# Sliding-window attention of the second block by pairs of heads, each pair behind its own query projection

## The chip, the cores and the metric

The kernel runs on one core of a Trainium2 chip. Of the core's engines TensorE (PE) does the matrix products, VectorE (DVE) and ScalarE (ACT) the element-wise work, GpSimd (POOL) a little of it, and SyncE (SP) issues most of the transfers. The metric is the device time of one execution in microseconds, the median of several runs.

## The reference, cut to what matters

Two blocks follow one another: the first with four branches (2 layers of it), the second with a feed-forward part, a mixer and another feed-forward part. The change lies in the mixer of the second block, with 512 positions and 1024 features:

```python
h = modulate(rms_norm_2(x, g_pre_mix[l]), sh2, sc2)
proj = h @ w_in[l]
q = proj[..., :D_ATTN].reshape(bsz, s, N_Q_HEADS, HEAD_DIM)            # 8 heads of 64
k = proj[..., D_ATTN:D_ATTN + D_KV].reshape(bsz, s, N_KV_HEADS, HEAD_DIM)   # 2 heads of 64
v = proj[..., D_ATTN + D_KV:D_ATTN + 2 * D_KV].reshape(bsz, s, N_KV_HEADS, HEAD_DIM)
u = proj[..., D_ATTN + 2 * D_KV:]                                      # 512 columns
attn = sliding_window_attention(q, k, v, attn_sinks[l])
ssm = s5_ssm(u, ...)
mixed = jnp.concatenate([rms_norm_2(attn, g_attn_out[l]), rms_norm_2(ssm, g_ssm_out[l])], axis=-1)
mixed = mixed @ w_out[l]
```

In the attention, each block of 128 queries reads its own block of 128 keys and the one before it (the first block only its own). A bias by distance is added, the maximum takes a sink in, and the softmax runs over the keys and the sink:

```python
m = jnp.maximum(jnp.max(scores, axis=-1, keepdims=True), sink)
p = jnp.exp(scores - m)
p = p / (jnp.sum(p, axis=-1, keepdims=True) + jnp.exp(sink - m))
out = jnp.einsum('bnkgqj,bnjkd->bnqkgd', p, vv)
```

The norm behind it (`rms_norm_2(attn, ...)`) runs over all 512 columns of a position, so over all eight heads. `s5_ssm` is a linear recurrence over the positions, with a GELU and a gate `y * sigmoid(y @ w_glu + b_glu)` behind it.

## The kernel before

Features lie on the partitions, positions along the free axis. A product of the large kind is split in three: an fp32 operand is kept as a rounded part and a remainder, and lines 258, 259 and 260 multiply high by high, low by high and high by low. The splits of the weights are made by ScalarE (L218) and VectorE (L219), from tiles `wr` into tiles `wh`, some of them with names of their own (`wa`).

The mixer of the second block is built in `block2`. First `mixer_in` projects `u` (tiles `ut`), `k` (`kd`), `v` (`vT`) and the first 128 columns of `q`, which are two heads. Then two generators are woven into one another, which means that the program text of one is emitted in steps between the steps of the other:

- `mixer`, the recurrence: four groups of products with `us` (L2347: 128 partitions, 64 moving columns, plain fp32), each followed by VectorE's multiplications and eight scans (L2348 to L2353); then four groups of output products (L2364 to L2366) with the GELU behind them; then the gate: products of `y2h` and `y2l` with a weight of 512 rows (lines 258 to 260, 512 columns), a tanh, L2397 and the splits L2405.
- `window_attention`: the three other projections of `q` (24 products with 512 columns each, two heads each), then a loop over the four blocks of queries. `scores(b)` makes the scores of all eight heads of a block (L2438, from `ho`, the keys, and `q`), adds the bias and takes the minimum of the negated scores on VectorE (L2441), and runs the softmax up to the reciprocal of the sum (`softmax_sink`). `values(b)` transposes the exponentials (L2453), copies them out of PSUM on ScalarE, multiplies them with the values (L2459) and scales by the reciprocal (L2462) into a tile `ot` of its block. `result(b)` squares and sums `ot` (L2469), takes a reciprocal square root by three Newton steps of short VectorE instructions (L2470, L268 to L275), scales (L2473), transposes (L2476) and splits the result (L2480 on ScalarE, L2481 on VectorE) into the tiles that the output projection reads. The three parts are staggered: scores of block i, values of block i - 1, result of block i - 2.

When both are done, `attended` multiplies the attention's columns with the first half of `w_out` (weights `wa` first). It begins with the columns of query blocks 0 and 1 and reads all eight heads. The other half of `w_out` follows.

The text's order is not the final one. A class `Plan` takes all instructions of the kernel, with costs and dependencies of its own, and writes a new order for every engine. What stands next to what on an engine is therefore read from the built kernel, as below, not from the text.

Of the kernel before, what the change touches and what calls it, by code (L numbers as in the profile page):

```python
# [11 lines left out]
F32 = mybir.dt.float32  # L12
# [4 lines left out]
AF = mybir.ActivationFunctionType  # L17
ALU = mybir.AluOpType
PSUM = bass.MemoryType.PSUM
DRAM = bass.MemoryType.DRAM  # L20
P = 128
NT = 528
NM = 16
# [13 lines left out]
KC = 8  # L37
BIG = 3.0e38
# [21 lines left out]
def free_bc(ap, n):  # L60

    return ap[:, :, None].to_broadcast([ap.shape[0], ap.shape[1], n])
# [57 lines left out]
class Net:  # L120
# [615 lines left out]
    def p_transposes(self, Ps, k0, n, pool, ch):  # L736
# [4 lines left out]
        for i in range(n):  # L741
            for h in range(2):
                nc.tensor.transpose(ps[:, (2 * i + h) * P:(2 * i + h + 1) * P], Ps[h][:, k0 + i * P:k0 + (i + 1) * P], self.ident)
        PT = pool.tile([P, 512], F32, tag=f"PT{ch}", name=f"PT_{self.n}", bufs=2)
        self.alt_copy(PT[:, :2 * n * P], ps[:, :2 * n * P])
        return PT.rearrange("p (i h q) -> p i h q", i=2, h=2)

# [12 lines left out]
    def pv_block(self, Ps, b_first, n_blocks, vt, vm, pool, kvs, ch=""):  # L760
# [5 lines left out]
        with self.in_turn():  # L766
            po = self.pst("o")
            for p in range(0, H, 2):
# [7 lines left out]
                for i in range(0, n_blocks, 2):  # L776
                    n = min(2, n_blocks - i)
                    PT = self.p_transposes(Ps[p:p + 2], NM + i * P, n, pool, ch)
                    if i == 0:
# [3 lines left out]
                    for k in range(n):  # L783
                        for s in range(2):
                            self.turn = nc.tensor.matmul(o[s], lhsT=vt[:, b_first + i + k, kv[s]:kv[s] + 64], rhs=PT[:, k, s], start=False,
                                                         stop=(i + k == n_blocks - 1), tile_position=(0, 64 * s), skip_group_check=True)
# [26 lines left out]
    def pv_meta(self, Pt, nk_blocks, vt, vm, r, pool, ch=""):  # L813
# [3 lines left out]
        with self.in_turn():  # L817
# [5 lines left out]
            for i in range(nk_blocks):  # L823
                nc.tensor.transpose(pt[:, i * P:(i + 1) * P], Pt[:, NM + i * P:NM + (i + 1) * P], self.ident)
            PT = pool.tile([P, 512], F32, tag=f"PT{ch}", name=f"PT_{self.n}", bufs=2)
            self.alt_copy(PT[:, :nk_blocks * P], pt[:, :nk_blocks * P])
# [984 lines left out]
class Net2(Net):  # L1811
# [598 lines left out]
    def window_attention(self, pool):  # L2410
        nc, I = self.nc, self.ins
        V, G = nc.vector, nc.gpsimd
        W = I["w_in_2"][0]
        kd, vT, q = self.kd, self.vT, self.q2
        vt = pool.tile([P, 4, P], F32, tag="vt2", name="vt2")
        ps = self.pst("t")
        for b in range(4):
            nc.tensor.transpose(ps[:, b * P:(b + 1) * P], vT[:, b * P:(b + 1) * P], self.ident)
        nc.scalar.copy(vt, ps.rearrange("p (b f) -> p b f", b=4))
        for c in range(1, 4):  # L2420
            self.mm(self.wload(W[:, P * c:P * c + P], KC), 0, self.ux, KC, NM, self.qev[c])
            yield
        bias = pool.tile([P, 2048], F32, tag="alibi", name="alibi").rearrange("p (h k) -> p h k", h=8)
        nc.sync.dma_start(bias, I["c_alibi"].rearrange("p (h k) -> p h k", h=8))
        sink = pool.tile([P, 8], F32, tag="sink2", name="sink2")
        nc.sync.dma_start(sink, I["attn_sinks_2"].to_broadcast([P, 8]))
        for c in range(4):
            self.mixed[c] = (self.xtile("u", F32R), self.xtile("u", F32R))
        def scores(b):
            k0, nk, b0 = (0, 128, 128) if b == 0 else (P * (b - 1), 256, 0)  # L2430
            nm = self.small(8, "nm8")
            sb = []
            for h in range(8):
                hp = (h % 2) * 64
                if h % 2 == 0:
                    bank = self.pst("s")
                s = bank[:, 256 * (h % 2):256 * (h % 2) + 256]
                nc.tensor.matmul(s[:, :nk], lhsT=q[h // 2][hp:hp + 64, b * P:(b + 1) * P], rhs=kd[h // 4][hp:hp + 64, k0:k0 + nk],  # L2438
                                 start=True, stop=True)
                t = pool.tile([P, 256], F32, tag="sb2", name=f"sb2_{b}{h}", bufs=15)  # L2440
                V.tensor_tensor_reduce(out=t[:, :nk], in0=s[:, :nk], in1=bias[:, h, b0:], scale=-1.0, scalar=BIG,  # L2441
                                       op0=ALU.add, op1=ALU.min, accum_out=nm[:, h:h + 1])
                sb.append(t)
            return sb, self.softmax_sink(sb, nk, nm, sink, 8, "W"), nk // P, k0 // P

        def values(b, sb, r, nb, kb):
            po = self.pst("o")
            for hh in range(0, 8, 2):
                pt = self.pst("t")
                for h in (hh, hh + 1):  # L2450
                    for i in range(nb):
                        o = (2 * (h - hh) + i) * P
                        nc.tensor.transpose(pt[:, o:o + P], sb[h][:, i * P:(i + 1) * P], self.ident)  # L2453
                PT = pool.tile([P, 2, 256], F32, tag="PT2", name=f"PT2_{b}{hh}", bufs=2)
                nc.scalar.copy(PT[:, :, :nb * P], pt.rearrange("p (h k) -> p h k", h=2)[:, :, :nb * P])
                for h in (hh, hh + 1):
                    kv = (h // 4) * 64
                    for i in range(nb):
                        nc.tensor.matmul(po[:, h * 64:h * 64 + 64], lhsT=PT[:, h - hh, i * P:(i + 1) * P],  # L2459
                                         rhs=vt[:, kb + i, kv:kv + 64], start=(i == 0), stop=(i == nb - 1))  # L2460
            ot = pool.tile([P, 512], F32, tag="ot2", name=f"ot2_{b}", bufs=2)
            V.tensor_tensor(out=ot.rearrange("p (h d) -> p h d", h=8), in0=po.rearrange("p (h d) -> p h d", h=8),  # L2462
                            in1=free_bc(r, 64), op=ALU.mult)
            return ot

        def result(b, ot):
            sq = pool.tile([P, 512], F32, tag="vT2", name=f"sqw{b}")
            v = self.small(1, "vw")
            nc.scalar.activation(sq, ot, AF.Square, accum_out=v)  # L2469
            V.tensor_scalar(out=v, in0=v, scalar1=1.0 / 512, scalar2=1e-6, op0=ALU.mult, op1=ALU.add)  # L2470
            rr = self.small(1, "rw")
            self.rsqrt(v, rr, 1)
            V.tensor_scalar(out=ot, in0=ot, scalar1=rr, scalar2=None, op0=ALU.mult)  # L2473
            ps = self.pst("t")
            for c in range(4):
                nc.tensor.transpose(ps[:, c * P:(c + 1) * P], ot[:, c * P:(c + 1) * P], self.ident)  # L2476
            for c in range(4):
                hi, lo = (t[:, NM + b * P:NM + (b + 1) * P] for t in self.mixed[c])
                p, g = ps[:, c * P:(c + 1) * P], self.col["g_attn_out"][:, c:c + 1]
                nc.scalar.activation(hi, p, AF.Copy, scale=g)  # L2480
                V.scalar_tensor_tensor(out=lo, in0=p, scalar=g, in1=hi.bitcast(F32), op0=ALU.mult, op1=ALU.subtract)  # L2481

        st, ot = {}, {}
        for i in range(6):
            if i < 4:
                st[i] = scores(i)
                yield
            if 0 < i < 5:
                ot[i - 1] = values(i - 1, *st[i - 1])
                yield  # L2490
            if i > 1:
                result(i - 2, ot[i - 2])
                yield

    def block2(self, taps=None):
        nc, I = self.nc, self.ins
# [580 lines left out]
```

## Time and profile before

| | |
|---|---|
| time, median of 3 runs | 3325.56 us (3321.98, 3325.56, 3337.65) |
| the profiled execution's own time | 3333.74 us |
| its span, first to last instruction | 3332.0 us |
| mean granted clock of TensorE | 0.948 |
| TensorE busy (products) | 3146.6 us, 94% |
| VectorE, ScalarE, GpSimd busy | 1856.6 us (56%), 1278.9 us (38%), 416.9 us (13%) |

The profile describes one execution. "Busy" says only that an engine was executing something; how fast TensorE went while busy is told by the granted clock, of which 1.0 is the full 2.4 GHz and 0.5 is 1.2 GHz. The end of a product is modelled, since products overlap in the engine; what one costs in a row of others is read from the start of one to the start of the next.

### The profile page before, as it was taken

To read this page: it belongs to the slowest core of one execution; us is meant where nothing else is said; L and a number is where in the kernel's file an instruction comes from. 1 tells how busy PE (TensorE), PEld (TensorE's weight loads), DVE (VectorE), ACT (ScalarE), POOL (GpSimd) and SP (SyncE) were. 2 spreads that over 40 slices of the span, in tenths; PEclk is the share of its full clock that TensorE was granted. 3 is DMA by queue.
4 is the path that set the end of the run, shared out by engine and by line. 5 is a ranking of instruction groups with operands and counts; after the bars stand their busy time and mean duration, and the time that the engine had idled before them with its cause. 6 is when DMAs were issued, how large, how long until landed. Compare 5 with 4: busy or idle time off the path is not lost. (4 is left out here: it accounts for less than half of the span.)

```text
span 3332.0 us, 57805 instructions
## 1 busy us (share of the span) xinstructions
PE 3146.6 (94%) x21892; PEld 2761.1 (83%) x21892; DVE 1856.6 (56%) x5062; ACT 1278.9 (38%) x2856; POOL 416.9 (13%) x444
## 2 busy tenths in 40 slices
PE   7888999999999988999999999999999999989997
PEld 6777888999999976877678887798888988888887
DVE  4466588754645857568965555853223634642224
ACT  2356444333332345654433232243323514433332
POOL 0101000011110011200002112411110201211101
PEclk9889999999999988999999999989999976889998
DMA  4721223343544652123344444572333543233343
GB/s 138 175 51 45 72 77 88 110 124 106 160 126 120 192 141 58 37 80 95 94 130 145 130 139 137 179 231 83 95 111 116 159 135 98 74 108 95 93 124 95
DMA packets 645883, 380.41 MB, mean 114 GB/s; under 512 B 66500, under 2 KB 613884, under 8 KB 645476
## 3 DMA queue, kind: packets, MB, share of 16 engines
q1 hardware_dynamic: 628520, 365.22, 37.6%
q0 software_dynamic: 13632, 9.61, 1.9%
q8 instruction: 172, 2.82, 0.4%
q10 hardware_dynamic: 3452, 1.89, 0.3%
q14 instruction: 107, 0.88, 0.1%
HBM read 333.16 MB, written 45.52 MB: 114 GB/s over the span
## 5 line engine op out<-in xcount | busy, mean ns | idle before, releaser
L258 PE MATMUL ps_mm<-u,wh 128*128 128x256 f32 (+2 forms) x2928 | 971.0, 333 | 16.8 <-ACT g L1514 4.4
L260 PE MATMUL ps_mm<-u,wh 128*128 128x256 f32 (+2 forms) x2928 | 963.6, 331 | 0.6 <-POOL u L231 0.3
L259 PE MATMUL ps_mm<-u,wh 128*128 128x256 f32 (+2 forms) x2912 | 956.7, 330 | 4.8 <-DVE wh L219 4.8
L258 PEld LDWEIGHTS ps_mm<-u,wh 128*128 128x128 f32 x2928 | 563.9, 193 | 74.1 <-issue 10.4
L219 DVE TENSOR_TENSOR wh<-wr,wh 128x512 fp32r<-128x512 f32 (+1 forms) x531 | 367.3, 703 | 460.3 <-issue 228.1
L218 ACT ACTIVATE wh<-wr 128x512 fp32r<-128x512 f32 (+1 forms) x588 | 354.9, 619 | 699.1 <-PE ps_mm L259 267.4
L260 PEld LDWEIGHTS ps_mm<-u,wh 128*128 128x128 f32 x2928 | 563.4, 193 | 50.7 <-issue 4.7
L259 PEld LDWEIGHTS ps_mm<-u,wh 128*128 128x128 f32 x2912 | 561.0, 193 | 53.5 <-DVE wh L219 6.2
L259 PE MATMUL ps_mm<-hid,wh 128*128 128x256 f32 (+2 forms) x988 | 298.3, 310 | 3.2 <-DVE wh L219 3.1
L258 PE MATMUL ps_mm<-hid,wh 128*128 128x256 f32 (+2 forms) x948 | 287.4, 312 | 2.8 <-ACT wh L218 2.8
L260 PE MATMUL ps_mm<-hid,wh 128*128 128x256 f32 (+2 forms) x948 | 287.1, 311 | 0.0
L1846 DVE SCALAR_TENSOR_TENSOR acc<-ho,cact,acc 128x128 f32<-128x128 f32 x504 | 186.4, 373 | 37.7 <-DMA ho<-in_w_ada_dram 30.1
L259 PEld LDWEIGHTS ps_mm<-hid,wh 128*128 128x128 f32 x988 | 184.4, 190 | 15.7 <-DVE wh L219 4.5
L258 PEld LDWEIGHTS ps_mm<-hid,wh 128*128 128x128 f32 x948 | 177.9, 191 | 13.4 <-ACT wh L218 3.0
L260 PEld LDWEIGHTS ps_mm<-hid,wh 128*128 128x128 f32 x948 | 177.6, 191 | 9.7 <-issue 0.4
L231 POOL TENSOR_TENSOR hid<-g,hid 128x512 fp32r<-128x512 f32 (+1 forms) x85 | 92.4, 1088 | 682.5 <-ACT hid L230 682.5
L218 ACT ACTIVATE wh<-wrx 128x512 fp32r<-128x512 f32 (+1 forms) x160 | 96.0, 601 | 205.0 <-PE ps_mm L260 100.8
L219 DVE TENSOR_TENSOR wh<-wrx,wh 128x512 fp32r<-128x512 f32 (+1 forms) x131 | 87.4, 667 | 136.7 <-issue 116.4
L88 POOL TENSOR_TENSOR na<-na,g 128x256 f32<-128x256 f32 (+2 forms) x62 | 63.1, 1018 | 778.8 <-issue 418.1
L258 PE MATMUL ps_mm<-u,hid 128*128 128x256 f32 (+1 forms) x448 | 135.2, 302 | 16.6 <-ACT hid L218 16.6
L259 PE MATMUL ps_mm<-u,hid 128*128 128x256 f32 (+1 forms) x448 | 135.0, 301 | 5.3 <-DVE hid L219 5.1
L260 PE MATMUL ps_mm<-u,hid 128*128 128x256 f32 (+1 forms) x448 | 133.7, 298 | 0.0
(589 smaller groups left out, 5674.8 us busy)
## 6 DMA issues: line engine op xcount, KB each, us to landing
wr<-in_w_in_dram SPq DMA_DIRECT2D x220, 256.0 KB
ho<-in_w_ada_dram SPq DMA_DIRECT2D x144, 256.0 KB
wr<-in_w_ffn_down_dram SPq DMA_DIRECT2D x80, 256.0 KB
wr<-in_w_down_dram SPq DMA_DIRECT2D x66, 256.0 KB
wr<-in_w_ffn_gate_dram SPq DMA_DIRECT2D x62, 256.0 KB
wr<-in_w_gate_dram SPq DMA_DIRECT2D x61, 256.0 KB
wr<-in_w_ffn_up_dram SPq DMA_DIRECT2D x60, 256.0 KB
wr<-in_w_up_dram SPq DMA_DIRECT2D x60, 256.0 KB
```

The lines of the kernel that those rows point to most:

```text
L88: nc.gpsimd.tensor_tensor(out=acc[:, a:b], in0=acc[:, a:b], in1=sq[:, a:b], op=ALU.add)
L218: self.last_split = nc.scalar.activation(hi[:, i:e], raw, AF.Copy)
L219: (nc.vector if o else eng).tensor_tensor(out=lo[:, i:e], in0=raw, in1=hi[:, i:e].bitcast(F32), op=ALU.subtract)
L231: (eng or self.nc.vector).tensor_tensor(out=lo, in0=x, in1=hi.bitcast(F32), op=ALU.subtract)
L258: T.matmul(o, lhsT=wh, rhs=xh[:, a:b], start=start, stop=False)
L259: T.matmul(o, lhsT=wl, rhs=xh[:, a:b], start=False, stop=False)
L260: T.matmul(o, lhsT=wh, rhs=xl[:, a:b], start=False, stop=stop)
L1846: V.scalar_tensor_tensor(out=acc, in0=w[:, k], scalar=c, in1=acc, op0=ALU.mult, op1=ALU.add)
```

## The change

The loops of the attention change places. The outer loop runs over the four pairs of heads, and the scores, the softmax and the values of a pair are made for all four blocks of queries at once. The projection of the next pair's queries stands behind the values of the pair before it, where all three stood ahead of the loop. The results need all heads of a block, so all four stand behind the loop. The sinks are copied once into a tile of 128 x 32 in the order in which the pairs use them. The finished values go into one tile `ot2` of four blocks by 512 columns, of which a pair writes 128 columns in every block.

```diff
-        for c in range(1, 4):
-            self.mm(self.wload(W[:, P * c:P * c + P], KC), 0, self.ux, KC, NM, self.qev[c])
-            yield
+        yield
...
+        sinks = pool.tile([P, 4, 4, 2], F32, tag="sinks", name="sinks")
+        V.tensor_copy(sinks, sink.rearrange("p (c h) -> p c h", h=2)[:, :, None, :].to_broadcast([P, 4, 4, 2]))
...
+        span = [(0, 128, 128)] + [(P * (b - 1), 256, 0) for b in range(1, 4)]
+
+        def scores(c):
+
             nm = self.small(8, "nm8")
             sb = []
-            for h in range(8):
-                hp = (h % 2) * 64
-                if h % 2 == 0:
-                    bank = self.pst("s")
...
+            for b, (k0, nk, b0) in enumerate(span):
+                bank = self.pst("s")
+                for i in range(2):
+                    h, hp = 2 * c + i, 64 * i
+                    s = bank[:, 256 * i:256 * i + 256]
+                    nc.tensor.matmul(s[:, :nk], lhsT=q[c][hp:hp + 64, b * P:(b + 1) * P], rhs=kd[h // 4][hp:hp + 64, k0:k0 + nk],
+                                     start=True, stop=True)
...
+        ots = pool.tile([P, 4, 512], F32, tag="ot2", name="ot2")
...
+            V.tensor_tensor(out=ots[:, :, P * c:P * (c + 1)].rearrange("p b (h d) -> p b h d", h=2),
+                            in0=po.rearrange("p (b h d) -> p b h d", b=4, h=2),
+                            in1=r.rearrange("p (b h) -> p b h", h=2)[:, :, :, None].to_broadcast([P, 4, 2, 64]), op=ALU.mult)
...
-        st, ot = {}, {}
-        for i in range(6):
-            if i < 4:
-                st[i] = scores(i)
+        st = None
+        for c in range(5):
+            new = scores(c) if c < 4 else None
+            yield
+            if c:
+                values(c - 1, *st)
                 yield
-            if 0 < i < 5:
-                ot[i - 1] = values(i - 1, *st[i - 1])
+            st = new
+            if c < 3:
+                self.mm(self.wload(W[:, P * (c + 1):P * (c + 2)], KC), 0, self.ux, KC, NM, self.qev[c + 1])
                 yield
-            if i > 1:
-                result(i - 2, ot[i - 2])
-                yield
+        for b in range(4):
+            result(b, ots[:, b])
+            yield
```

What this does to the order on TensorE is seen at three places. Each row is one instruction or several alike ("x4"): its line, operation, the tile written and the tiles read, and the size of the output. The first place is the end of the three projections, before the change. `ps_mm_29996` is the third later projection, `ps_s` a score tile, `us` the recurrence's input.

```order
L260 MATMUL ps_mm_29996<-u_28744,wh_29986 128x512
L258 MATMUL ps_mm_29996<-u_28745,wh_29986 128x512
L2438 MATMUL ps_s_30075<-ho_29370,q_0_29373 128x128
L259 MATMUL ps_mm_29996<-u_28745,wh_29987 128x512
L260 MATMUL ps_mm_29996<-u_28746,wh_29986 128x512
L2347 MATMUL ps_mm_29965<-us,wh_29963 128x64 x7
L2438 MATMUL ps_s_30082<-ho_29370,q_1_29374 128x128
L2438 MATMUL ps_s_30089<-ho_29371,q_2_29375 128x128
L2438 MATMUL ps_s_30096<-ho_29371,q_3_29376 128x128
```

Here the last products of the third projection have passed, and the scores of query block 0 (128 columns, with all four tiles of `q`) stand between the first groups of the recurrence. The place that answers to it after the change is the start of the second later projection, `ps_mm_30229`.

```order
L2440 MATMUL ps_s_29909<-ho_29370,q_0_29373 128x256
L2440 MATMUL ps_s_30059<-ho_29370,q_1_29374 128x256
L2347 MATMUL ps_mm_30185<-us,wh_30183 128x64 x8
L2440 MATMUL ps_s_30066<-ho_29370,q_1_29374 128x256
L2418 MATMUL ps_t_29855<-misc,vT_29372 128x128 x4
L2347 MATMUL ps_mm_30198<-us,wh_30196 128x64 x8
L258 MATMUL ps_mm_30229<-u_28731,wh_30219 128x512
L259 MATMUL ps_mm_30229<-u_28731,wh_30220 128x512
L260 MATMUL ps_mm_30229<-u_28732,wh_30219 128x512
```

All four groups with `us` now stand ahead of the second projection, and between them stand scores of the first and the second pair, `q_0` and `q_1` (256 columns for all blocks but the first). The second place is the end of the third later projection after the change, `ps_mm_30472`.

```order
L258 MATMUL ps_mm_30472<-u_28745,wh_30462 128x512
L259 MATMUL ps_mm_30472<-u_28745,wh_30463 128x512
L260 MATMUL ps_mm_30472<-u_28746,wh_30462 128x512
L2469 MATMUL ps_t_30389<-misc,sb_12_30061 128x128 x2
L2469 MATMUL ps_t_30389<-misc,sb_13_30064 128x128 x2
L2364 MATMUL ps_mm_30498<-us,wh_30499 128x64
```

The third projection, with 24 products, has moved behind three of the four groups of output products; behind it transposes of the second pair's exponentials (heads 2 and 3) and the fourth group of output products follow. The third place is on VectorE, at the end of the attention. Before the change, it shows the values of the last query block (`ot_3`) and what follows.

```order
L2462 TENSOR_TENSOR ot_3_30810<-ps_o_30765,rW_30605 128x512
L273 TENSOR_TENSOR rt_5359_30849<-ry_5360_30850 128x1
L219 TENSOR_TENSOR wh_31099<-wr_31100,wh_31098 128x512
L274 TENSOR_TENSOR rt_5359_30849<-rt_5359_30849,rv_5358_30848 128x1
L219 TENSOR_TENSOR wh_31099<-wr_31104,wh_31098 128x512
L275 SCALAR_TENSOR_TENSOR rw_30847<-rt_5359_30849,ry_5360_30850 128x1
L2405 SCALAR_TENSOR_TENSOR u_30820<-g_30818,gs,u_30819 128x8x32
L2473 TENSOR_SCALAR ot_2_30663<-ot_2_30663,rw_30847 128x512
L2470 TENSOR_SCALAR vw_30918<-vw_30918 128x1
```

Here only the results of blocks 2 and 3 follow (the square roots of block 2 are in progress above), with splits of weights and the gate's splits. After the change, the same place begins with the values of the last pair, L2477.

```order
L2477 TENSOR_TENSOR ot_29886<-ps_o_30701,rW_30569 128x4x128
L219 TENSOR_TENSOR wh_30809<-wr_30810,wh_30808 128x512
L2397 SCALAR_TENSOR_TENSOR g_30647<-g_30647,yf 128x512
L2485 TENSOR_SCALAR vw_30775<-vw_30775 128x1
L268 TENSOR_SCALAR rv_5346_30779<-vw_30775 128x1
L269 TENSOR_SCALAR rt_5347_30780<-vw_30775 128x1
L270 TENSOR_SCALAR ry_5348_30781<-rt_5347_30780 128x1
L273 TENSOR_TENSOR rt_5347_30780<-ry_5348_30781 128x1
L274 TENSOR_TENSOR rt_5347_30780<-rt_5347_30780,rv_5346_30779 128x1
L2405 SCALAR_TENSOR_TENSOR u_30649<-g_30647,gs,u_30648 128x8x32
L275 SCALAR_TENSOR_TENSOR ry_5348_30781<-rt_5347_30780,ry_5348_30781 128x1
L2397 SCALAR_TENSOR_TENSOR g_30676<-g_30676,yf 128x512
```

Behind the last values, the result of the first block only begins (L2485 with the square root's steps), and the gates L2397 and their splits L2405 stand between its steps; the results of the three other blocks follow.

## Rows read from the trace of the kernel before

**Rows 1.** Page, 40 slices of the span: tenths of the granted clock.

```profile
PEclk9889999999999988999999999989999976889998
```

**Rows 2.** Stretches: length; busy PE, PEld, DVE, ACT, POOL; clock; DMA share; GB/s.

```profile
2673.30:2698.90 25.60, 25.57 (x138) 21.06 (x136) 6.28 (x27) 4.50 (x7) 0.89 (x1) 1.00 0.47 151
2698.90:2797.90 99.00, 99.00 (x398) 85.24 (x397) 34.92 (x120) 24.44 (x76) 12.24 (x13) 0.50 0.36 111
2797.90:2811.50 13.60, 11.53 (x66) 7.95 (x65) 4.95 (x23) 7.88 (x26) 1.27 (x1) 1.00 0.03 11
2811.50:2818.40 6.90, 6.90 (x25) 6.03 (x25) 5.57 (x18) 5.60 (x12) 1.19 (x1) 0.51 0.12 40
2818.40:2828.60 10.20, 7.57 (x51) 6.55 (x50) 6.94 (x20) 7.75 (x17) 1.85 (x2) 1.00 0.46 132
2828.60:2843.65 15.05, 11.36 (x48) 10.35 (x49) 10.92 (x39) 8.33 (x18) 0.00 (x0) 0.50 0.72 225
2673.30:2843.65 170.35, 161.93 (x718) 137.18 (x717) 69.58 (x243) 58.50 (x154) 17.44 (x17) 0.65 0.38 117
```

**Rows 3.** Timeline of TensorE at full clock: start, duration, instruction.

```profile
2798.34 0.39 PE L259 MATMUL ps_mm<-y2h,wh 128*128 128x512 f32 x1
2798.57 0.40 PE L258 MATMUL ps_mm<-y2h,wh 128*128 128x512 f32 x1
2798.90 0.70 PE L2438 MATMUL ps_s<-ho,q 64*128 64x256 f32 x2
2799.52 0.50 PE L259 MATMUL ps_mm<-y2h,wh 128*128 128x512 f32 x1
...
2821.76 0.60 PE L2476 MATMUL ps_t<-misc,ot 128*128 128x128 f32 x4
2822.20 0.60 PE L2453 MATMUL ps_t<-misc,sb 128*128 128x128 f32 x4
...
2825.12 1.00 PE L2459 MATMUL ps_o<-vt,PT 128*128 128x64 f32 x8
2825.96 0.33 PE L97 MATMUL ps_q<-misc,na 128*128 128x1 f32 x2
```

**Rows 4.** Timeline of TensorE, where the clock fell.

```profile
2695.22 0.71 PE L2438 MATMUL ps_s<-ho,q 64*128 64x128 f32 x6
...
2696.33 0.70 PE L2438 MATMUL ps_s<-ho,q 64*128 64x256 f32 x4
2696.96 1.10 PE L2347 MATMUL ps_mm<-us,wh 128*128 128x64 f32 x8
```

**Rows 5.** Timeline of TensorE, where the clock rose again.

```profile
2787.40 5.38 PE L2459 MATMUL ps_o<-vt,PT 128*128 128x64 f32 x24
2792.54 0.77 PE L258 MATMUL ps_mm<-y2h,wh 128*128 128x512 f32 x1
...
2797.80 0.47 PE L260 MATMUL ps_mm<-y2l,wh 128*128 128x512 f32 x1
```

**Rows 6.** Timeline of TensorE: last values, first product of the output projection.

```profile
2830.55 3.51 PE L2459 MATMUL ps_o<-vt,PT 128*128 128x64 f32 x16
...
2843.65 0.55 PE L258 MATMUL ps_mm<-u,wa 128*128 128x256 f32 x1 [1.50 <-DVE nv L107]
```

**Rows 7.** Timeline of VectorE between 2824 and 2837 us.

```profile
2824.07 0.35 DVE L2481 SCALAR_TENSOR_TENSOR u<-ps_t,col,u 128x128 fp32r<-128x128 f32 x1
2824.33 0.15 DVE L270 TENSOR_SCALAR ry<-rt 128x1 int32<-128x1 int32 x1
...
2834.10 0.69 DVE L2462 TENSOR_TENSOR ot<-ps_o,rW 128x512 f32<-128x512 f32 x1 [2.50 <-PE ps_o L2459]
2834.71 0.15 DVE L273 TENSOR_TENSOR rt<-ry 128x1 f32<-128x1 f32 x1
2834.78 0.68 DVE L219 TENSOR_TENSOR wh<-wr,wh 128x512 fp32r<-128x512 f32 x1
...
2836.71 0.48 DVE L2473 TENSOR_SCALAR ot<-ot,rw 128x512 f32<-128x512 f32 x1
```

More of the change, by code (lines that the diff above doesn't have):

```diff
@@ L2426, in window_attention @@
         nc.sync.dma_start(sink, I["attn_sinks_2"].to_broadcast([P, 8]))
+        sinks = pool.tile([P, 4, 4, 2], F32, tag="sinks", name="sinks")
+        V.tensor_copy(sinks, sink.rearrange("p (c h) -> p c h", h=2)[:, :, None, :].to_broadcast([P, 4, 4, 2]))
         for c in range(4):
             self.mixed[c] = (self.xtile("u", F32R), self.xtile("u", F32R))
-        def scores(b):
-            k0, nk, b0 = (0, 128, 128) if b == 0 else (P * (b - 1), 256, 0)
+        span = [(0, 128, 128)] + [(P * (b - 1), 256, 0) for b in range(1, 4)]
@@ L2431, in scores @@
+        def scores(c):
             nm = self.small(8, "nm8")
             sb = []
-            for h in range(8):
-                hp = (h % 2) * 64
-                if h % 2 == 0:
-                    bank = self.pst("s")
[L2437 to L2443, printed above, removed]
@@ L2444, in scores @@
-            return sb, self.softmax_sink(sb, nk, nm, sink, 8, "W"), nk // P, k0 // P
-        def values(b, sb, r, nb, kb):
+            for b, (k0, nk, b0) in enumerate(span):
[5 more added lines that the diff above has]
+                                     start=True, stop=True)
+                    t = pool.tile([P, 256], F32, tag="sb2", name=f"sb2_{b}{h}", bufs=15)
+                    V.tensor_tensor_reduce(out=t[:, :nk], in0=s[:, :nk], in1=bias[:, h, b0:], scale=-1.0, scalar=BIG,
+                                           op0=ALU.add, op1=ALU.min, accum_out=nm[:, 2 * b + i:2 * b + i + 1])
+                    sb.append(t[:, :nk])
@@ new lines, in scores @@
+            sk = sinks[:, c].rearrange("p b h -> p (b h)")
+            ng, den, es, r = (self.small(8, n) for n in ("ngW", "denW", "esW", "rW"))
+            V.scalar_tensor_tensor(out=ng, in0=sk, scalar=-1.0, in1=nm, op0=ALU.mult, op1=ALU.min)
+            for h, t in enumerate(sb):
+                nc.scalar.activation(t, t, AF.Exp, bias=ng[:, h:h + 1], scale=-1.0, accum_out=den[:, h:h + 1])
+            V.tensor_tensor(out=es, in0=sk, in1=ng, op=ALU.add)
+            nc.scalar.activation(es, es, AF.Exp)
@@ L2447, in values @@
+            V.tensor_tensor(out=r, in0=den, in1=es, op=ALU.add)
+            V.reciprocal(out=r, in_=r)
+            return sb, r
+        ots = pool.tile([P, 4, 512], F32, tag="ot2", name="ot2")
+        def values(c, sb, r):
             po = self.pst("o")
-            for hh in range(0, 8, 2):
+            kv = (c // 2) * 64
+            for b, (k0, nk, _) in enumerate(span):
+                nb = nk // P
                 pt = self.pst("t")
[L2450 to L2464, printed above, removed]
+                for i in range(2):
+                    for j in range(nb):
+                        o = (2 * i + j) * P
+                        nc.tensor.transpose(pt[:, o:o + P], sb[2 * b + i][:, j * P:(j + 1) * P], self.ident)
@@ new lines, in values @@
+                PT = pool.tile([P, 2, 256], F32, tag="PT2", name=f"PT2_{c}{b}", bufs=2)
+                nc.scalar.copy(PT[:, :, :nk], pt.rearrange("p (h k) -> p h k", h=2)[:, :, :nk])
+                for i in range(2):
+                    o = (2 * b + i) * 64
+                    for j in range(nb):
+                        nc.tensor.matmul(po[:, o:o + 64], lhsT=PT[:, i, j * P:(j + 1) * P], rhs=vt[:, k0 // P + j, kv:kv + 64],
+                                         start=(j == 0), stop=(j == nb - 1))
```

## The prediction

> **What bounds the kernel now.** I read the slices of the page first. TensorE's granted clock stands near ten tenths almost everywhere; the deepest dip, to seven and six tenths, lies in the 33rd and 34th of the 40 slices of 83.3 us, 2666 to 2832 us [rows 1], and that is the mixer of the second block, the only place that the change touches. Then I cut this place into stretches at the moments when the clock changed [rows 2]. From 2673.30, where the query projections of the later pairs begin, to 2843.65, where the output projection over the attention's columns begins, 170.35 us pass and TensorE is busy for 161.93 of them, so it waits for only 8.4 us. The reader is to see the column of the clock: full for 25.60 us, then 0.50 for 99.00 us in which TensorE is busy all the time, then changing four more times. The half-clock stretches add up to 120.95 us with 117.3 us of busy time. At full clock the same work would take half of that, so 58.6 us are lost to the clock, against 8.4 us lost to waiting. The rest, 170.35 - 58.6 - 8.4, is 103 us of work at full clock. VectorE is busy for 69.6 of these 170 us and ScalarE for 58.5, so the stage is TensorE's, at half speed.
>
> The order of the work around the two changes of the clock comes next. The clock fell at 2698.9, behind twelve records of score products among products with 64 moving columns [rows 4] (a product in fp32 leaves two records). It stayed down while TensorE ran nothing but score products, transposes and products with 64 columns. It rose at 2797.9, behind nine products with 512 columns, which had come in behind and among the records with 64 [rows 5].
>
> Prices at full clock, from start to start [rows 3]: 0.23 us for a product with 512 columns; 0.62 for a score product with 256 columns that stands alone, 0.63 / 2 = 0.31 in a row of them [rows 4]; 0.44 / 4 = 0.11 for a transpose; 0.84 / 8 = 0.105 for a record with 64 columns, so 0.21 a product. At half clock the 24 records from 2787.40 to 2792.54 take 0.214 each, twice as much [rows 5].
>
> **The change, part by part.** The products, transposes, exponentials and evictions are the same in number and shape, and so is the attention's softmax: 32 score tiles with the same widths, four passes of eight. New are one small copy for the sinks and a strided view for the four multiplications that finish the values; both have as many or fewer elements than what stands there (512 per partition and pass), and VectorE is free for about half of the stage, so I price them at nothing; uncovered they would cost under 1 us.
>
> *The projections.* Before, the three projections (72 products of 0.23, 16.6 us at full clock) run back to back at full clock. After, the first stands close behind, the second only after the last group of products with `us`, the third in the middle of the products of the state's outputs. Two of them now meet a half clock. What that costs: the clock in rows 5 rose behind nine such products, so I let ten of the 24 run at half, 10 x 0.23 = 2.3 us lost each, 4.6 for both. What it gives back is the clock for what stands behind. The trace shows how long a full clock lasted once it had risen in this stage: 13.60 and 10.20 us, both times ended where TensorE also waited for other engines (11.53 busy of 13.60; 7.57 of 10.20) [rows 2].
>
> The walk through the new order, in us of work at full clock. The first projection and the products with `us` around it keep the full clock for some 15. Then nine score products stand among 32 products with `us`, much like rows 4: 9 x 0.31 + 32 x 0.21 = 9.5 us of work at half, 9.5 lost. The second projection lifts the clock (2.3 lost), and some 16 us behind it run full, until the score products of the third pair stand ahead of the third projection: 8 us of work at half, 8 lost. The third projection lifts it again (2.3 lost), and the last quarter of the state's outputs, the last scores and the products with `y2` follow. That is 22 us lost instead of 58.6. The bounds: if a rise holds no longer than the shortest one, 10.2 us, then 15 + 2 x 10.2 of the 90.7 us up to the last values run full, the rest at half except the few products of `y2`: 48 lost. If products with 64 columns keep a full clock that they have been given, only the scores bring it down: 10 lost. I take 22 since the stretch that fell [rows 4] held as many score records as others, and most of the new stretches hold fewer.
>
> *Waits.* The work comes faster, so its feeders are closer. In the 99.00 us at half clock VectorE is busy for 34.92 and ScalarE for 24.44 [rows 2]; the same in some 65 us is 54% and 38%, and neither becomes the bound over the whole. Locally VectorE comes closer: each of the four groups of products with `us` asks it for four instructions over 512 elements, 0.6 us each from start to start [rows 7], and eight scans, with the score tiles between them. The last softmax must also pass its exponentials before its transposes. I take 10 us of idle TensorE up to the last values, against 8.4 now; bounds 5 and 20.
>
> *The tail.* This is what the change makes worse. Before, the results of query blocks 0 and 1 are done among other work, and from the end of the last values (2834.06, [rows 6]) to the output projection (2843.65) 9.6 us pass. After, no block has all its heads before the last pair is done, so all four results stand behind it on VectorE, with the gates of the state and the splits of weights among them. Up to the scaling of block 2, whose transposes stand ahead of the first product of the output projection, the order has 22 long instructions of 0.6 us from start to start, 3 scalings of 0.4 (the row shows 0.48 with its overlap), 8 subtractions of 0.27 and some 39 short ones of 0.07 [rows 7]: 13.2 + 1.2 + 2.2 + 2.7 = 19.3 us, and 0.5 for four transposes: 20. TensorE has 36 products with `y2` (8.3 us), transposes, sums and twelve narrow products for this time, 12.6 us in all, so it waits for VectorE. Bounds: 15 if the gates' instructions fall behind the results, 25 if the short ones wait for each other.
>
> *Transfers.* The same tiles are loaded; the weights of the later projections go past the first tiles of `dE` on SP's queue, which come earlier, and each group of `us` needs 1.5 MB with its tables. At 225 GB/s the transfers were busy for 0.72 of the time [rows 2], so I estimate 310 GB/s at full use and some 5 us a group, against 7 us of its 16 products of 0.21 and of the scores and projections between them: hidden, and within the 10 us of waits where not.
>
> *Sum.* Work up to the last values 103 - 12.6 = 90.7; lost to the clock 22; waits 10; tail 20: 142.7 us instead of 170.35. That is 28 us less, on the profiled execution's own time (3333.74) 3306. This execution is 8.2 us above the median of the three shown (3325.56); on that scale the forecast is **3298 us**. With all good bounds it is 90.7 + 10 + 5 + 15 = 120.7 (-50, 3276), with all bad ones 90.7 + 48 + 20 + 25 = 183.7 (+13, 3339).
>
> **Rivals.**
> *The clock follows nothing that the change moves.* If two bursts are too little, or what lowers the clock lies in the score products and 64-column products wherever they stand, the loss stays in proportion: 58.6 x 90.7 / 103 = 51.6, waits 8.4, tail 20: 170.7 us, the same time, 3326. For it speaks that the clock stayed down for 99.00 us of full work; against it, that the clock rose at 2797.9 behind nine wide products. The Trainium skill has a rule of this kind (TensorE: Matmul & The Clock Gate, Why this matters for your kernels): the clock is kept by not leaving TensorE idle between bursts. By that rule the change would do nothing for the clock, since TensorE is never idle in that stretch, and would not have fallen there at all; the trace does not agree, 99.00 busy of 99.00 at 0.50 [rows 2], so the kind of work counts too.
>
> *Waits in place of the half clock.* TensorE gets faster and stands before VectorE's evictions and scans, and each stop lowers the clock again, as at 2811.5 and 2828.6. With 20 us of waits and 35 lost the sum is 90.7 + 35 + 20 + 20 = 165.7: 5 us gained, 3321. For it speaks that both later falls came with waits.
>
> *Slower: the wide products lose their full clock and lift nothing.* Now 72 of them run at 1.0. If the second and third run at half throughout, 11 us are lost on them, and of the 90.7 us only the first 15 run full: 75.7 lost, waits 5, tail 20: 191.4, 21 us more, 3347. It decides once more than 170.35 - 90.7 - 5 - 20 = 54.7 us are lost to the clock. Against it stands the rise of 2797.9, which came under wide products [rows 5].
>
> **How the numbers follow.** No change is what stays within 0.5% of the median, 16.6 us, about what a measurement of this kernel can tell. The forecast with its bounds gets 0.64 (of it 0.04 below a gain of 16.6), the clock that does not follow 0.14, waits in its place 0.12, slower 0.10. So faster 0.62 (0.60 from the forecast, 0.02 from the better part of the waits), same 0.28, slower 0.10. The range goes from 3274, just past the good bounds, to 3326, which takes in both cases of no change; its upper end leaves out the slower case and the worst bounds, the lower end very little. The likeliest case alone spans 3276 to 3312.
>
> **What would show it.** In the changed profile, the stretch between the first wide products and the output projection should show a full clock for well over half of it, with rises inside the second and third projection and falls at groups of score products. The output projection should begin near 2816 instead of 2843.65; from the last values to it some 20 us, with VectorE busy nearly all the time; waits of TensorE about 10 us ahead of the last values. The prediction is wrong if the clock stays at 0.50 behind the second projection, if TensorE waits for VectorE or for `wh` tiles for more than 20 us, or if the tail is above 25.

## The result and the profile after

The changed kernel took 3293.7 us (median of 6, 3289.15 to 3297.11) against 3327.23 us of the kernel before (median of 6, 3321.65 to 3337.65, three of them the runs shown ahead of the prediction): a ratio of 0.9889, 95% interval 0.9868 to 0.991, so about 1% faster. The forecast was 3298 us.

The slices of the changed kernel's page, tenths of the granted clock, which answer to [rows 1]:

```profile
PEclk9899999999999988899999999989999999889998
```

The dip to seven and six tenths in the 33rd and 34th slice is gone. The same stage cut into stretches, as in [rows 2] (length; busy PE, PEld, DVE, ACT, POOL; clock; DMA share; GB/s). It begins at 2681.11, where the projections of `mixer_in` end, as the stretch from 2673.30 did before the change.

```profile
2681.11:2775.69 94.58, 92.14 (x643) 78.01 (x642) 46.78 (x154) 39.11 (x112) 14.47 (x15) 1.00 0.52 158
2775.69:2784.50 8.81, 8.42 (x36) 6.48 (x35) 8.15 (x22) 8.15 (x16) 1.90 (x1) 1.00 0.22 69
2784.50:2788.00 3.50, 1.10 (x8) 0.86 (x8) 2.36 (x10) 3.22 (x7) 1.27 (x1) 1.00 0.76 223
2788.00:2806.60 18.60, 7.99 (x32) 6.94 (x33) 14.09 (x62) 9.03 (x22) 0.00 (x0) 0.51 0.55 170
```

Up to the end of the last values (2775.69) the clock is at 1.00 for all 94.58 us, and TensorE waits for 2.4 of them. Then comes a tail of 30.91 us, with VectorE busy for 24.6 of it, TensorE for 17.5, and the clock at half for the last 18.6. The stage takes 2806.60 - 2681.11 = 125.49 us instead of 170.35, which is 44.9 less. From the output projection to the end both need the same: 488.60 us after, 488.35 before. The two spans differ by only 36.8 because the changed kernel's profiled execution reached the stage 7.8 us later. Up to there TensorE runs the same products in the same order in both, and three profiled executions of the changed kernel itself came to this point at 2681.11, 2682.70 and 2670.62; this difference is between executions, not between kernels.

### The profile page after: what moved, and what is told of

Read it like the earlier page. It is cut to its first block, busy times and chain, and to the rows that moved or that the text cites. A ratio compares the mean times of both kernels' runs of the same rounds, so it can differ in the third digit from the quotient of the medians.

```text
span 3295.2 us, 57803 instructions
## 1 busy us (share of the span) xinstructions
PE 3096.8 (94%) x21892; PEld 2717.5 (82%) x21892; DVE 1857.9 (56%) x5063; ACT 1277.6 (39%) x2856; POOL 418.2 (13%) x444
## 5 line engine op out<-in xcount | busy, mean ns | idle before, releaser
L231 POOL TENSOR_TENSOR hid<-g,hid 128x512 fp32r<-128x512 f32 (+1 forms) x85 | 92.4, 1087 | 684.6 <-ACT hid L230 684.6
L259 PE MATMUL ps_mm<-u,hid 128*128 128x256 f32 (+1 forms) x448 | 133.6, 298 | 5.2 <-DVE hid L219 5.1
```

What stands on the lines that cost most here:

```text
L231: (eng or self.nc.vector).tensor_tensor(out=lo, in0=x, in1=hi.bitcast(F32), op=ALU.subtract)
L259: T.matmul(o, lhsT=wl, rhs=xh[:, a:b], start=False, stop=False)
```

## The experiments

The numbers of all profiled executions first, in us, read from their timelines: from the end of the projections of `mixer_in` (`u`, `k`, `v` and the first pair's `q`; this point is read to within 0.2 us) to the last values, from there to the first product of the output projection (the tail), and both together. Below, wide products are those with 512 columns (the projections and the products with `y2`), and narrow work is the rest of the stage: scores, transposes and products with 64 columns.

| kernel | to the last values | tail | stage | clock ahead of the last values |
|---|---|---|---|---|
| before | 160.8 | 9.6 | 170.4 | half for 99.0, 6.9 and 5.5 |
| changed | 94.6 | 30.9 | 125.5 | full |
| changed, second execution | 95.7 | 30.6 | 126.2 | half for 3.4 |
| changed, third execution | 93.6 | 30.6 | 124.1 | full |
| all projections in front, four executions | 92.5, 92.4, 92.8 and 133.6 | 29.5 to 30.1 | 122.0, 122.1, 122.9 and 163.3 | full, full, full; half for 88.5 |
| third projection in front | 93.2 | 29.5 | 122.7 | full |
| second projection in front | 112.9 | 31.8 | 144.7 | half for 40.9 |
| before, two extra projections | 140.1 | 5.6 | 145.7 | half for 34.1 and about 12 |
| before, results at the end | 134.9 | 22.7 | 157.6 | half for 80.4 |
| one root, two executions | 94.5 and 94.3 | 19.3 and 18.8 | 113.8 and 113.0 | full |

**All projections in front of the pairs.** This keeps pairs and late results and takes away only the place of the projections.

```diff
+        for c in range(1, 4):
+            self.mm(self.wload(W[:, P * c:P * c + P], KC), 0, self.ux, KC, NM, self.qev[c])
+            yield
...
-            if c < 3:
-                self.mm(self.wload(W[:, P * (c + 1):P * (c + 2)], KC), 0, self.ux, KC, NM, self.qev[c + 1])
-                yield
```

> The changed kernel, with the three later projections put back in front of the pairs; pairs, values and results as changed. Theory (the wide products of the second and third projection, standing among the narrow ones, keep the clock up): without them the clock falls at the first scores among the products with us and stays at 0.50 up to the products with y2, as before the change; some 45 to 55 us are lost, so about 3293.7 + 45 = 3339 us, or 10 above the kernel before, since the long tail stays. Rival (scores of one pair stand in ones and twos among other products, where those of a query block stood in longer rows, and this alone keeps the clock): clock near 1.0 between the projections and the last values, 3294 us within 8.

Measured: median 3319.12 of 10 executions against 3333.59 of the kernel before, ratio 0.9946 (0.9921 to 0.9971). Neither theory was right as it stood. Three executions lay at 3292 to 3299 us, seven at 3314 to 3328, none between, and the profile was of one of the three: its clock was at 1.00 for all 92.5 us up to the last values. So narrow work can run at full clock with no wide product in it, and yet seven of ten executions took some 25 us more. The same kernel was run again to profile one of those:

> All three projections in front of the pairs once more, for a profile of another execution: in the first round three of ten executions lay at 3292 to 3299 us, seven at 3314 to 3328. Theory (the slow ones are those in which the clock fell among the narrow products and stayed down until the products with y2): if this profile is of an execution above 3310 us, it shows a long stretch at 0.50 between the products with us and those with y2, some 25 to 50 us of it lost; if it is of one below 3300, a full clock. Rival (the slow executions lose their time in waits or elsewhere in the program): a slow one shows a full clock in the mixer.

> All three projections in front of the pairs, one execution with its profile, to see one of the slow ones (9 of 17 so far lie above 3313 us, 8 below 3299). Theory: above 3313 us the clock falls among the products with us and stays at 0.50 for 45 to 70 us, up to the products with y2; below 3299 it stays at 1.0. Rival: a slow execution with a full clock in the mixer, its time lost elsewhere.

> The same kernel, a second execution with its profile, for the same question and with the same expectations.

The first of these gave 3293.45 us (7 executions, ratio 0.9896, 0.986 to 0.9932), five below 3299 and two above 3331, and the profile again had a full clock. The two single executions gave 3330.4 us and 3297.32 us. Of 19 executions of this kernel 9 lie below 3300 us and 10 above 3313. The stretches of the execution of 3330.4 us (columns as above):

```profile
2677.55:2715.40 37.85, 37.17 (x208) 29.55 (x208) 16.52 (x60) 9.12 (x25) 2.88 (x3) 1.00 0.59 190
2715.40:2803.90 88.50, 88.50 (x370) 77.70 (x370) 26.07 (x88) 25.25 (x74) 9.66 (x11) 0.50 0.27 87
2803.90:2811.15 7.25, 7.25 (x63) 6.97 (x62) 1.93 (x4) 3.71 (x11) 1.27 (x1) 1.00 0.13 38
2811.15:2840.86 29.71, 18.93 (x82) 15.12 (x80) 24.93 (x90) 21.02 (x45) 3.10 (x2) 0.72 0.53 160
```

And of the execution of 3297.32 us, the same program:

```profile
2683.59:2776.37 92.78, 92.27 (x638) 78.50 (x637) 44.53 (x151) 37.80 (x108) 13.97 (x15) 1.00 0.52 165
2776.37:2806.44 30.07, 19.67 (x80) 15.78 (x80) 24.91 (x90) 21.01 (x45) 3.11 (x2) 0.69 0.52 158
```

One program, one order, equal tails: 163.31 us and 122.85. In the first the clock falls at 2715.4, TensorE stays busy for 88.50 of 88.50 us at 0.50, and the clock rises at 2803.9 behind five products with `y2`. That is 44 us lost by the row, and 40.5 us by the difference of the stages. So the theory held, but the half clock lasted longer than the 45 to 70 us that were expected. What stood ahead of the fall, in the timeline of TensorE:

```profile
2712.64 0.70 PE L2442 MATMUL ps_s<-ho,q 64*128 64x256 f32 x2
2713.97 0.70 PE L2442 MATMUL ps_s<-ho,q 64*128 64x256 f32 x2 [0.63 <-DVE nm L2445]
2714.59 4.67 PE L2347 MATMUL ps_mm<-us,wh 128*128 128x64 f32 x23
```

Scores, a wait of 0.63 us for VectorE's score reduction, scores, products with `us`. The execution of 3297.32 us had the same wait, 0.46 us long, and its clock did not fall.

**Two extra projections in the kernel before.** By query blocks, all later projections in front, and two of them computed again into a tile that nobody reads (work that the reference does not need).

```diff
+            if i in (1, 2):
+                spare = pool.tile([P, 512], F32, tag="spare", name=f"spare{i}", bufs=2)
+                self.mm(self.wload(W[:, P * (i + 1):P * (i + 2)], KC), 0, self.ux, KC, NM,
+                        lambda ps, a, b, t=spare: nc.scalar.activation(t[:, a - NM:b - NM], ps, AF.Copy, scale=0.125))
+                yield
```

> The kernel before, by query blocks, with two projections computed a second time into a tile that nobody reads, one behind the values of block 0 and one behind those of block 1: 48 wide products more, 11 us at full clock. Theory (wide products among the narrow ones lift the clock): the clock rises inside each of the two, and of the 58.6 us lost to the clock some 20 to 30 are left: 3327 - 33 + 11 = 3305 us, faster than before although it does more. Rival (the order of the scores sets the clock): the clock is down around both, 3327 + 11 to 22 = 3338 to 3349 us.

Measured: 3303.81 us (4 executions), ratio 0.9909 (0.9876 to 0.9941). More work, and 30 us faster.

```profile
2678.24:2714.03 35.79, 34.91 (x218) 29.69 (x217) 15.19 (x56) 9.42 (x27) 3.01 (x3) 1.00 0.63 202
2714.03:2748.10 34.07, 33.75 (x110) 24.96 (x110) 13.91 (x52) 6.64 (x23) 4.04 (x4) 0.50 0.30 93
2748.10:2808.00 59.90, 57.57 (x369) 47.67 (x369) 33.78 (x97) 36.44 (x92) 9.98 (x10) 0.98 0.40 122
```

The clock falls as in the kernel before, but rises at 2748.1 in the middle of the first extra projection and then holds for some 58 us of narrow work by query blocks, with the second extra projection and the products with `y2` among it. So wide products ended a fall in this order of the attention too.

**One of the two projections in front.** The changed kernel, with `c` = 3 or `c` = 2 moved in front beside the first.

```diff
-            if c < 3:
+            if c < 2:
```

> The changed kernel with the third later projection put in front of the pairs beside the first; the second stays between the products with us and the outputs of the state. Theory (the clock can fall among the products with us, in some executions and not in others, and once down it stays down until wide products come): the second projection ends every such fall after at most some 30 us of work, so the time stays near that of the changed kernel, at most 8 us above it on this chip, with executions close together. Rival (place of the projections does not matter, executions of the pairwise order vary by themselves): the same spread as with all projections in front, 3292 to 3328 us, and the same median as there.

```diff
-            if c < 3:
+            if c in (0, 2):
```

> The changed kernel with the second later projection put in front of the pairs beside the first; the third stays where the change put it, in the middle of the outputs of the state. Theory (a fall among the products with us lasts until the next wide products): some 40 us of narrow work lie between the products with us and the third projection, so an execution that falls loses 20 to 25 us and one that does not loses nothing: median between the changed kernel and the kernel with all projections in front, some 3300 to 3312 us on this chip. Rival (place does not matter): as with all projections in front, about 3319 us.

> The changed kernel once more, on the chip of these runs, for its spread. Theory (the second and third projection end every fall): all executions within some 12 us, 3290 to 3305 us, none above 3310; the profile shows a full clock, or a half clock that ends inside a projection. Rival (the first profile of the changed kernel was a lucky one and the projections do nothing): executions on both sides of 3305, as with all projections in front (3292 to 3299 and 3314 to 3328).

Measured on one chip: third in front 3293.12 us (0.9883, 0.9861 to 0.9906; 3288.06 to 3296.75), second in front 3315.01 us (0.994, 0.9919 to 0.9961; 3305.48 to 3318.34), the changed kernel 3296.42 us (0.9884, 0.9862 to 0.9906; 3286.8 to 3298.62). The third projection makes no difference that these runs show; the second, directly behind the products with `us`, does. Without it there (second in front):

```profile
2672.65:2704.30 31.65, 30.78 (x192) 25.33 (x190) 15.27 (x57) 7.38 (x22) 2.54 (x2) 1.00 0.65 216
2704.30:2745.20 40.90, 40.90 (x156) 33.50 (x157) 14.83 (x54) 8.73 (x26) 4.03 (x4) 0.50 0.28 86
2745.20:2785.58 40.38, 40.38 (x299) 35.53 (x299) 14.85 (x42) 21.60 (x61) 6.93 (x8) 1.00 0.35 109
```

The fall comes among the products with `us` and lasts 40.90 us, to the third projection, where the clock rises behind six wide products: 20 us lost, and the median is 19 us above that of the changed kernel. It is also above the 3300 to 3312 us that the theory gave, since none of the six executions lies below 3305 us; of the seven with all projections in front, on the same chip, five lay below 3299. So as far as so few executions tell, the place of the projections also changes how often the clock falls, and no run here shows why. The second execution of the changed kernel shows a fall too, within the first products of the second projection, which then ends it:

```profile
2682.70:2710.90 28.20, 26.54 (x184) 22.45 (x183) 17.26 (x57) 7.24 (x21) 3.79 (x4) 1.00 0.71 232
2710.90:2714.30 3.40, 3.40 (x10) 2.19 (x8) 2.79 (x11) 0.68 (x2) 0.94 (x1) 0.50 0.20 76
2714.30:2778.35 64.05, 63.40 (x453) 54.14 (x453) 26.87 (x87) 31.20 (x89) 9.72 (x11) 1.00 0.42 126
```

Here it lasts 3.40 us and costs 1.7. Its timeline around the fall, and then that of the changed kernel's first profile at the same place in the program:

```profile
2706.68 1.90 PE L2347 MATMUL ps_mm<-us,wh 128*128 128x64 f32 x16
2710.03 0.47 PE L258 MATMUL ps_mm<-u,wh 128*128 128x512 f32 x1 [1.45 <-DVE zin L2348]
...
2710.80 0.54 PE L258 MATMUL ps_mm<-u,wh 128*128 128x512 f32 x1
2711.13 0.63 PE L259 MATMUL ps_mm<-u,wh 128*128 128x512 f32 x1
...
2714.68 0.50 PE L260 MATMUL ps_mm<-u,wh 128*128 128x512 f32 x1
```

```profile
2705.09 1.90 PE L2347 MATMUL ps_mm<-us,wh 128*128 128x64 f32 x16
2708.59 0.47 PE L258 MATMUL ps_mm<-u,wh 128*128 128x512 f32 x1 [1.60 <-DVE zin L2348]
2708.89 0.40 PE L259 MATMUL ps_mm<-u,wh 128*128 128x512 f32 x1
```

A wait of 1.45 us before a fall in the one, of 1.60 without a fall in the other. What decides in a single execution stays open.

**Results at the end, by query blocks.**

```diff
-            if i > 1:
-                result(i - 2, ot[i - 2])
-                yield
+        for b in range(4):
+            result(b, ot[b])
+            yield
```

> The kernel before, by query blocks, with the results (norm, transposes, splits) of all four blocks put behind the last values, as the change does. It prices the tail by itself. Theory (the tail of four results is VectorE's and costs some 20 us more than before): from the last values to the output projection 28 to 32 us instead of 9.6, and 3327 + 12 to 20 = 3339 to 3347 us, since TensorE has fewer interruptions ahead of it. Rival (the tail after the change is long for other reasons, such as the weights' splits or transfers): below 18 us there, and 3327 us within 8.

Measured: 3319.07 us (10 executions, 3287.23 to 3330.69), ratio 0.9936 (0.9908 to 0.9964): faster than before, where both sides expected the same or slower. The tail grew as it should, from 9.6 to 22.7 us, less than the theory's 28. But the last values came 26 us earlier in the stage (134.9 against 160.8), partly because the results' own work had moved behind them; the whole stage is 12.8 us shorter. In the kernel before, the results of the first blocks stand between the clock's rise at 2797.9 and the last values, and TensorE waits there and falls twice [rows 2]; without them the clock, once risen, held at 0.96 up to the last values, and the first fall lasted 80.4 us instead of 99.0:

```profile
2716.10:2796.50 80.40, 80.40 (x325) 68.37 (x325) 26.51 (x86) 21.75 (x63) 10.81 (x12) 0.50 0.34 103
2796.50:2818.68 22.18, 21.86 (x149) 18.52 (x148) 11.83 (x46) 15.43 (x41) 0.64 (x2) 0.96 0.13 37
```

Its median is that of the pairs with all projections in front, on the same chip (3319.07 and 3319.12), and both spread over some 35 to 43 us. On another chip the same pairs had a median of 3293.45 us: where the executions fall into two groups, a median of ten or seven says mostly how many fell, and what the pairs add by themselves is not shown.

**One root for the tail.** The squares of a pair are summed behind its values, and one root serves all four blocks.

```diff
+            for b in range(4):
+                sq = pool.tile([P, 128], F32, tag="sqw", name=f"sqw{c}{b}", bufs=2)
+                nc.scalar.activation(sq, ots[:, b, P * c:P * (c + 1)], AF.Square, accum_out=sums[:, c, b:b + 1])
...
-            rr = self.small(1, "rw")
-            self.rsqrt(v, rr, 1)
+            rr = self.small(4, "rw")
+            self.rsqrt(v, rr, 4)
```

> The changed kernel, with the squares of a pair summed behind the pair's values (16 squares over 128 columns on ScalarE for 4 over 512) and one square root for all four blocks behind the last pair, where four stood: 36 short VectorE instructions fewer. Theory (the tail is bound by VectorE's row of four roots with their steps, which wait for one another): 31 us from the last values to the output projection fall to some 22, 3285 us. Rival (the tail is bound by the splits of weights and the transfers): the tail stays above 28 and the time within 4 us of 3293.7.

> The changed kernel with one square root for all four blocks, once more, beside the changed kernel on one chip. Theory (the tail behind the last values is VectorE's row of roots): 7 to 11 us below the changed kernel, tail 19 to 21 us. Rival (the first reading of 3288 us was the chip's): within 4 us of it.

> The changed kernel, as the measure for the kernel with one square root on the same chip. Theory: 3292 to 3298 us, no execution above 3305, the clock at 1.0 from the first later projection to the last values but for at most some 10 us that end in the second projection. Rival (its executions vary as those with all projections in front): some above 3310.

Measured: 3287.98 us (6 executions, 0.9861, 0.983 to 0.9892), then on another chip 3287.67 us (0.9858, 0.9835 to 0.9882) beside 3290.74 us of the changed kernel (0.9865, 0.9846 to 0.9883; 3283.55 to 3294.14, none above 3305). The tail fell as expected:

```profile
2681.39:2775.65 94.26, 94.09 (x649) 80.62 (x648) 47.62 (x155) 43.71 (x138) 14.39 (x15) 1.00 0.50 154
2775.65:2794.40 18.75, 12.80 (x55) 10.74 (x55) 16.02 (x39) 13.63 (x32) 3.54 (x2) 0.77 0.73 218
```

12 us less in the tail, so VectorE's row of roots, with the sums that they wait for, made it (the edit moves both). But the rest of the program took 491.5 us where the changed kernel took 488.6 and 486.8, probably since more of the results is left to be made beside the output projection, which was not tested. Of the 12 us some 3 to 5 go there. On one chip the medians differ by 3 us, within the intervals, where the theory had 7 to 11 and the rival at most 4: this version is no slower than the changed kernel, and that it is faster is not shown.

## Why the prediction was right

The total was right, and so was its main mechanism: the loss at half clock was what the change removed. But three of its terms ended outside their bounds, two below and one above, and by its own sign (a tail above 25 us) the prediction was wrong in the tail.

| term, us | forecast | changed kernel, first profile |
|---|---|---|
| work to the last values | 90.7 | 92.1 |
| lost to the clock ahead of the last values | 22 (10 to 48) | 0; 1.7 in the second execution |
| waits ahead of the last values | 10 (5 to 20) | 2.4 |
| tail | 20 (15 to 25) | 30.9 |
| stage | 142.7 | 125.5 |

That the total came within 5 us is in good part luck. The stage shrank by 44.9 us where 28 were forecast. Of the 17 us between, 7.8 went by ahead of the stage in the changed kernel's profiled execution, and about 5 are due to the median: this execution lay 3.3 us above that of its kernel, where the forecast took off 8.2.

*The clock.* The walk let the clock fall at each group of scores among narrow products, because the scores of [rows 4] stood ahead of a fall. That step failed, and so did the reading that the kind of work brings the clock down: the same work ran at either level. In three profiles with all projections in front, TensorE ran nothing but scores, transposes and products with 64 columns for some 60 us at full clock (2707.42, the last projection, to 2767.74, the first product with `y2`, in the first of them). In every profile that lost the clock ahead of the last values the first fall came among the groups with `us` or just behind them, in some executions and not in others; what the half clock then cost was the distance to the next wide products: 88.5 us with none, 40.9 to the third projection, 3.4 to the second. That the second and third projection lift the clock was right; that both have to, was not.

*The tail.* It ended outside its bounds. The sum of VectorE's instructions up to the scaling of block 2 was 19.3 us; it took 26.2 (2775.72 to 2801.91). And I let the output projection begin there, which it did not. The end of the tail on VectorE, then on TensorE:

```profile
2802.10 0.15 DVE L268 TENSOR_SCALAR rv<-vw 128x1 f32<-128x1 f32 x1
2802.17 0.14 DVE L269 TENSOR_SCALAR rt<-vw 128x1 int32<-128x1 int32 x1
2802.35 0.15 DVE L270 TENSOR_SCALAR ry<-rt 128x1 int32<-128x1 int32 x1
2802.53 0.16 DVE L273 TENSOR_TENSOR rt<-ry 128x1 f32<-128x1 f32 x1
...
2806.23 0.15 DVE L275 SCALAR_TENSOR_TENSOR rw<-rt,ry 128x1 f32<-128x1 f32 x1
2806.30 0.15 DVE L107 TENSOR_SCALAR nv<-ps_q 128x2 f32<-128x2 f32 x1
```

```profile
2802.05 1.11 PE L2491 MATMUL ps_t<-misc,ot 128*128 128x128 f32 x4 [1.67 <-DVE vw L2485]
2806.60 0.55 PE L258 MATMUL ps_mm<-u,wa 128*128 128x256 f32 x1 [3.43 <-DVE nv L107]
```

A step that needs the one before it starts 0.18 us behind it (2802.17 to 2802.35), where steps that do not depend on each other stand 0.07 apart. The first product waits 3.43 us for L107, which reads the sums (`ps_q`) out of PSUM, in banks that `ps_mm` shares there, and stands in VectorE's row behind the whole root of block 3. The order shows that, and [rows 6] had the same wait, of 1.50 us, in the kernel before; I read only the transposes. What L107 costs by itself was not tested: with all projections in front the same product waits 2.05 us, put down to a split of ScalarE, and the tail is only 0.5 to 1.4 us shorter. Of the 6.9 us ahead of that, 4.6 are VectorE's waits for ScalarE, the longest 1.61 us for a split of weights. That the roots and their sums make the tail was tested (18.75 us with one root).

*Waits and transfers.* TensorE's 2.4 us of waits ahead of the last values were for VectorE (1.60 and 0.19, both behind products with `us`) and ScalarE (0.55); none for a transfer. The place was as forecast, the size was a quarter.

*The rivals.* That the clock follows nothing that the change moves is refuted by the medians with the second projection in front and behind (3315.01 and 3296.42 us). The waits did take some of the gain, in the tail instead of ahead of it. The slower case fell: in no profile of the changed kernel did a wide burst run at half to its end.

What the parts are worth: late results by query blocks -14.5 us by the medians on one chip; what pairs add to that is not shown. The second projection behind the groups with `us` is worth another 20 to 45 us in those executions that would fall (3313.66 to 3338.2 us with all projections in front); all 16 executions of the changed kernel lie between 3283.55 and 3298.62 us.

## What to carry to other kernels

Where profiles show the clock falling ahead of a stretch of narrow products, keep a block of wide products that is due anyway and put it directly behind that place: here it bounded what a fall cost (3.4 us at half clock, against 40.9 and 88.5 with the next wide products farther off). One profile of a kernel with such a stretch says little; the spread of the executions gives a hint whether the clock fell in some of them. And when a tail is summed from one engine's row, look also for what the next stage's first product needs besides data, such as a PSUM bank that a late instruction frees; what moving that instruction would save was not tested here.

## What was not expected of the hardware

The same program in the same order ran 92.78 us of work at 1.00 in one execution and lost 44 us to 0.50 in another, with none of 19 executions between 3300 and 3313 us. In the six profiles that fell among the products with `us` or just behind them, TensorE had stood waiting for VectorE just before in five (0.48, 0.63, 0.87, 0.88 and 1.45 us); in the kernel before there was no such wait, only scores. Waits of 0.46, 0.57, 1.60 and 1.83 us at such places went by without a fall. What decides it stays open. The Trainium skill (TensorE: Matmul & The Clock Gate, Why this matters for your kernels) ties drops to idle gaps between bursts, longer than any wait named here. The traces do not bear that out as the whole of it: five falls came behind waits of 1.45 us or less and one behind none, and in 88.50 us busy of 88.50 at 0.50 narrow work did not bring the clock back before products with `y2` stood among it.
